# Input norm and HGRN value projection of a hybrid encoder trunk: one hand-written order, first channel halves of all token tiles ahead of the second

## The chip, the cores and the metric

The kernel runs on 1 core of one Trainium2 chip. The metric is device time in microseconds (us) of one execution; a comparison uses the median of several runs of each kernel. TensorE (PE, with its weight loads as PEld) does the matmuls and transposes, VectorE (DVE) and ScalarE (ACT) the elementwise work, GpSimd (POOL) some small operations, SyncE (SP) issues most DMAs.

## The reference, cut to what matters

One layer of an encoder: x (512 tokens x 1024 channels, float32) goes through a token mixer (HGRN2 heads and mLSTM heads), cross-attention over 256 memory tokens and a squared-ReLU MLP. The change touches only its beginning, the norm of the input and one block of columns of the input projection:

```python
def rmsnorm(x, g):
    y = x32 * lax.rsqrt(jnp.mean(x32 * x32, axis=-1, keepdims=True) + NORM_EPS)
    return (y * g.astype(jnp.float32)).astype(x.dtype)

# token_mixer(rmsnorm(x, norm_mix), ...)
proj = xn @ w_in + b_in            # w_in: 1024 x 4624
(h_q, h_f_fwd, h_f_bwd, h_i, h_g, m_q, m_k, m_v, m_o, ...) = split_cols(proj, IN_SPLITS)
v_h = to_heads(h_i, HGRN_HEADS)    # h_i: columns 1536 to 2047, the HGRN values
```

## The kernel before, in words

Every float32 matrix product is done as three matmuls on a high and a low part (L236, L237, L238): high by high, high by low, low by high. So each operand is first split: ACT copies it rounded (the high part), DVE subtracts that from the original (the low part). This is `split_out` (L232 on ACT, L233 on DVE).

Weights stream from one packed array in 512 KB slices. `load(i)` issues slice i on SP's queue into one of 3 buffers `st`; `split(i)` makes its pair `wh`, `wl`, of which there are also 3. The value projection uses slices 0 to 3: slice q holds the 256 input channels 2q and 2q+1 (in units of 128) for all 512 output columns. Slice 4 is that of the gates, slices 5 and on are those of the next projections.

The input norm works by token tiles t = 0 to 3 (128 tokens each) and channel halves g = 0, 1 (512 channels each). For a tile: ACT squares and sums it (L301), DVE (L172) and POOL (L174) make 1/rms; for each half, DVE scales it by 1/rms and by the gain (L306, the scale), PE turns it with four 128x128 transposes against the identity, which lies in the constants `cs` (L309, the turn), ACT and DVE split the result into `xT[g]` (L232, L233). The gain row is spread over the partitions by two small matmuls (L144) into `gmix`, two of the four PSUM banks of the pool `mm`. The value projection (`proj_t`, called behind the norm) takes four more banks of that pool, one for each token tile. Each (tile, slice) piece is six 128x512 matmuls: two channel blocks by three products. Slices 0 and 1 need `xT[0]` of that tile, slices 2 and 3 need `xT[1]`.

What sets the order: the program text is only a wish. A scheduler in the tile framework orders each engine's instructions by priority and by its own idea of when inputs are ready; the scale, the turn and the split are written under high priority. It is decided when the program is built. On the chip each engine then runs its own list strictly in that order, and waits on semaphores for the others. `small_setup` (masks, small constants, `selr` at L162 and L163) is also placed by that scheduler.

Of the kernel before, what the change touches and what calls it, by code (L numbers as in the profile page):

```python
# [13 lines left out]
AF = mybir.ActivationFunctionType  # L14
ALU = mybir.AluOpType
# [3 lines left out]
P = 128  # L19
S = 512  # L20
D = 1024
# [58 lines left out]
def trunk(ctx: ExitStack, tc: tile.TileContext, x, mem, wpk, vec, cst, lmask, rmask, rows, out):  # L80
# [5 lines left out]
    v, sc, gp, pe = nc.vector, nc.scalar, nc.gpsimd, nc.tensor  # L86
    cnt = [0]

    def nm(s):
        cnt[0] += 1  # L90
        return f"{s}_{cnt[0]}"

    def T(tag, w, bufs, dt=F32):
        return (sb if w == 516 else big).tile([P, w], dt, tag=tag, name=nm(tag), bufs=bufs)

    def mmb():
        return psm.tile([P, 512], F32, tag="mm", name=nm("mm"))

    def smb():
        return pss.tile([P, 512], F32, tag="sm", name=nm("sm"))  # L100

    def tiny(w):
        return sb.tile([P, w], F32, tag=f"tiny{w}", name=nm("tiny"), bufs=2 if w == 8 else 6)

    def ap(t, off, *dims):
        a = t[:, :]
        return bass.AP(a.tensor, a.offset + off, [list(a.ap[0])] + [list(d) for d in dims])
# [16 lines left out]
    ident = cs[:, C_ID:C_ID + P]  # L124
    grow1 = RG()
    xin = [A16(), A16()]
    xtile = [xin[t // 2][:, (t % 2) * 1024:(t % 2) * 1024 + 1024] for t in range(4)]
# [6 lines left out]
    def load_x(t):  # L134
        nc.sync.dma_start(out=xtile[t], in_=x[t * P:t * P + P, :])
# [3 lines left out]
    nc.scalar.dma_start(out=cs, in_=cst[:, 0:NC1])  # L139
    one1 = misc[0:1, 63:64]  # L140
    gp.memset(one1, 1.0)
    gmix = [mmb(), mmb()]
    for g in range(2):
        pe.matmul(gmix[g], lhsT=one1.to_broadcast([1, P]), rhs=grow1[0:1, g * 512:g * 512 + 512], start=True, stop=True)  # L144

    def small_setup():
        lmf = A4()
        nc.sync.dma_start(out=vc, in_=vec)
        nc.sync.dma_start(out=lmf[:, 0:len(LEVELS) * P], in_=lmask)
        for j in range(2):  # L150
            a = lmf[64 * j:64 * j + 64, 64 * j:NLV * P]
            v.tensor_copy(lm[64 * j:64 * j + 64, :].rearrange("p (l t) -> p l t", t=64),
                          bass.AP(a.tensor, a.offset, [list(a.ap[0]), [P, NLV], [1, 64]]))
        le, lr = tiny(8), tiny(8)
        lg = vc[:, V_LB:V_LB + 8]
        v.tensor_tensor(out=le, in0=lg, in1=lg, op=ALU.subtract)
        sc.activation(le, le, AF.Exp)
        v.reciprocal(lr, le)
        v.tensor_tensor(out=le, in0=le, in1=lr, op=ALU.mult)
        v.tensor_tensor(out=lb[:, 0:8], in0=le, in1=le, op=ALU.subtract)  # L160
        v.tensor_scalar(out=lb[:, 8:16], in0=lb[:, 0:8], scalar1=-1.0, scalar2=1.0, op0=ALU.mult, op1=ALU.add)
        v.tensor_copy(selr[0:64, :], cs[0:64, C_SEL:C_SEL + 8])  # L162
        v.tensor_copy(selr[64:128, :], cs[0:64, C_SEL:C_SEL + 8])  # L163
        v.tensor_scalar(out=negb, in0=vc[:, V_FF:V_FF + 8], scalar1=-1.0, scalar2=None, op0=ALU.mult)
# [5 lines left out]
    def rstd_of(ss, w, n):  # L170
        ms = tiny(w)
        v.tensor_scalar(out=ms, in0=ss, scalar1=1.0 / n, scalar2=EPS, op0=ALU.mult, op1=ALU.add)  # L172
        r = tiny(w)
        gp.tensor_tensor(out=r, in0=ms, in1=nh.to_broadcast([P, w]), op=ALU.pow)  # L174
        return r, ms
# [7 lines left out]
    def tick():  # L183
        for _ in range(rate[0]):
            tick1()
# [19 lines left out]
    st_tiles, hl_tiles = {}, {}  # L205

    def load(i):
        if i >= NSTREAM or i in st_tiles:
            return
        t = T("st", 1024, 3)  # L210
        nc.sync.dma_start(out=t, in_=wpk[i])
        st_tiles[i] = t

    def split(i):
        if i >= NSTREAM or i in hl_tiles:
            return
        load(i)
        s = st_tiles[i]
        hi, lo = T("wh", 1024, 3, F32R), T("wl", 1024, 3, F32R)
        split_out(hi, lo, s)  # L220
        hl_tiles[i] = (hi, lo)

    def weights(key):
        i = SIDX[key]
        with (tc.high_priority() if i > 2 else ExitStack()):
            for n in range(i, i + 3):
                split(n)
            load(i + 3)
        return hl_tiles[i]

    def split_out(dst_hi, dst_lo, src):
        sc.activation(dst_hi, src, AF.Copy)  # L232
        v.tensor_tensor(out=dst_lo, in0=src, in1=dst_hi.bitcast(F32), op=ALU.subtract)  # L233

    def mm3(ps, ah, al, bh, bl, first, last):
        pe.matmul(ps, lhsT=ah, rhs=bh, start=first, stop=False)  # L236
        pe.matmul(ps, lhsT=ah, rhs=bl, start=False, stop=False)  # L237
        pe.matmul(ps, lhsT=al, rhs=bh, start=False, stop=last)  # L238


    def xk(tiles, n=512):
        o = []
        for k in range(8):
            t = tiles[k // 4]
            b = (k % 4) * 2 * n
            o.append((t[:, b:b + n], t[:, b + n:b + 2 * n]))
        return o

    def proj_d(mat, c0, xs, n=512, count=2):

        for j in range(count):
            wh, wl = weights(("d", mat, 0, c0 + P * j))
            ps = mmb()
            for k in range(8):
                z = slice(k * P, k * P + P)
                mm3(ps[:, :n], wh[:, z], wl[:, z], xs[k][0], xs[k][1], k == 0, k == 7)
                if k == 3:
                    tick()
            yield ps
            tick()  # L260

    def proj_t(mat, k0, c0, xs, ntile=4, pre=None, late=False):

        acc = [mmb() for _ in range(ntile)]

        def part(t, q, w):
            for k in range(2):
                kk = 2 * q + k
                xh, xl = xs[kk][0][:, t * P:t * P + P], xs[kk][1][:, t * P:t * P + P]
                z = slice(k * 512, k * 512 + 512)  # L270
                mm3(acc[t], xh, xl, w[0][:, z], w[1][:, z], kk == 0, kk == 7)

        for q in range(2 if late else 3):
            w = weights(("t", mat, k0 + 2 * q, c0))
            for t in range(ntile):
                part(t, q, w)
                if t % 2 == 1:
                    tick()
        if pre is not None:
            pre()  # L280
        tail = [(q, weights(("t", mat, k0 + 2 * q, c0))) for q in range(2 if late else 3, 4)]
        for t in range(ntile):
            for q, w in tail:
                part(t, q, w)
            yield t, acc[t]
            if t % 2 == 1:
                tick()


    xT = XT()  # L290
    load(0)
    load_x(1)
    load_x(2)
    load(1)
    load_x(3)

    junk = G4()
    for t in range(4):
        xt = xtile[t]
        ss = tiny(1)  # L300
        sc.activation(junk, xt, AF.Square, accum_out=ss)  # L301
        r, _ = rstd_of(ss, 1, D)
        with tc.high_priority():
            for g in range(2):
                xg = xt[:, g * 512:g * 512 + 512]
                v.scalar_tensor_tensor(out=xg, in0=xg, scalar=r, in1=gmix[g], op0=ALU.mult, op1=ALU.mult)  # L306
                ps = smb()
                for k in range(4):
                    pe.transpose(ps[:, k * P:k * P + P], xg[:, k * P:k * P + P], ident)  # L309
                p3 = ps[:, :].rearrange("p (k t) -> p k t", t=P)  # L310
                split_out(ap(xT[g], t * P, [1024, 4], [1, P]), ap(xT[g], 512 + t * P, [1024, 4], [1, P]), p3)
        if t < 2:
            split(t)
    small_setup()
    xs = xk(xT)


    vh = []
# [1 line left out]
    def bias_row(i):  # L320
        b = T2()
        nc.sync.dma_start(out=b[:, 0:512], in_=rows[1 + i // 2:2 + i // 2, (i % 2) * 512:(i % 2) * 512 + 512].to_broadcast([P, 512]))
        return b

    bvh = bias_row(0)
    for t, ps in proj_t("in", 0, 1536, xs):
        d = VV()
        v.tensor_tensor(out=d[:, 0:512], in0=ps, in1=bvh[:, 0:512], op=ALU.add)
        vh.append(d)
# [431 lines left out]
    for t in range(2):  # L761
# [6 lines left out]
        ss = tiny(1)  # L768
        v.tensor_tensor(out=ss, in0=s2_[:, 0:1], in1=s2_[:, 1:2], op=ALU.add)
        r, _ = rstd_of(ss, 1, D)  # L770
# [6 lines left out]
    for k in range(8):  # L777
        ps = smb()
        for t in range(2):
            pe.transpose(ps[:, t * P:t * P + P], mt[t][:, k * P:k * P + P], ident)  # L780
        g = vc[:, V_MEM + k:V_MEM + k + 1]
# [224 lines left out]
    for f in range(4):  # L1006
# [3 lines left out]
        for p in range(4):  # L1010
            a = []
            for j in range(2):
                ps, = proj_d("up", 1024 * f + P * (p + 4 * j), x3, count=1)
# [49 lines left out]
        def ahead(n):  # L1063
            with tc.high_priority():
                for m in range(n, n + 3):
                    job(f, m)
                i = max(hl_tiles)
                for m in range(i + 1, i + 4):
                    load(m)
            if n == 8 and f < 3:  # L1070
                sum_loads(f + 1, ("U", "T3"))
            return job(f, n)
# [6 lines left out]
        while n < len(JOBS):  # L1079
            p, g = JOBS[n]  # L1080
# [8 lines left out]
            w = ahead(n)  # L1089
# [95 lines left out]
```

## Time and profile before

| | |
|---|---|
| median of 3 runs (lowest to highest) | 861.75 us (860.46 to 863.5) |
| the profiled execution: its own time | 861.91 us |
| its span, first to last instruction | 860.1 us |
| PE busy in the span | 840.4 us (98%) |
| DVE, ACT, POOL busy | 566.6, 423.7, 67.4 us |
| mean granted TensorE clock | 0.995 of full |
| first matmul of the value projection | 11.32 us after the span's start |

The kernel is bound by PE nearly everywhere. A row of the timeline gives start, duration, engine, line, operation, output and input, count, and in brackets how long the engine was idle just before and what ended that. PE's rows overlap, since matmuls are pipelined: what counts there is the distance from one start to the next, not the duration of one row.

### The profile page before, as it was taken

The page shows a single profiled execution, that of the slowest core. Times are in us where ns is not written, and L with a number is a line of the kernel's source. Part 1 is how long each engine was busy: PE and PEld are TensorE (multiplying, and loading weights), DVE is VectorE, ACT ScalarE, POOL GpSimd, SP SyncE. Part 2 cuts the span into 40 slices and gives each one's busy share as a digit, 9 for nine tenths or more (in the row PEclk, how much of TensorE's full clock was granted, in tenths as well). Part 3 has the DMA queues.
Part 4 walks back from the last instruction along what each step waited for, and adds up shares of the span by engine and source line. Part 5 has one row for each costly group of instructions (what it writes and reads, how often), then busy time and mean ns, then how long its engine had stood idle before and what let it go on. Part 6 is the DMA issues. An engine that isn't in the chain of part 4 may idle for free.

```text
span 860.1 us, 11677 instructions
## 1 busy us (share of the span) xinstructions
PE 840.4 (98%) x4438; PEld 693.8 (81%) x4438; DVE 566.6 (66%) x996; ACT 423.7 (49%) x773; POOL 67.4 (8%) x114
## 2 busy tenths in 40 slices
PE   7999999998999999999999999999999999999995
PEld 5888788887987987888888887888888888888884
DVE  5558874599347987654545446676667656856675
ACT  5336454445558576454443346553454344434544
POOL 1000000100010000100001200003101210220001
PEclk9999999999999999999999999999999999999998
DMA  7332223122152232452213852348935993698322
GB/s 265 123 119 75 73 80 136 46 94 76 50 147 74 99 123 99 158 135 98 74 50 110 206 149 76 97 130 229 282 118 127 275 259 99 173 284 203 123 50 98
DMA packets 32682, 113.62 MB, mean 132 GB/s; under 512 B 3761, under 2 KB 3889, under 8 KB 32626
## 3 DMA queue, kind: packets, MB, share of 16 engines
q1 hardware_dynamic: 23120, 78.84, 26.9%
q0 software_dynamic: 9216, 33.56, 17.7%
q8 instruction: 35, 0.57, 0.3%
q10 hardware_dynamic: 290, 0.47, 0.2%
q14 instruction: 21, 0.17, 0.1%
HBM read 110.76 MB, written 2.10 MB: 131 GB/s over the span
## 4 chain that ended last, share of the span: by engine, by line
PE 85%; issue 6%; DVE 5%; DMA 1%; ACT 1%; POOL 1%; POOLq 0%; ACTq 0%; DVEq 0%
PE mm L236 19%; PE mm L237 19%; PE mm L238 18%; PE sm L1059 5%; PE sm L1060 5%; PE sm L1061 5%; PE sm L688 2%; PE sm L673 2%; PE sm L454 2%; DVE wl L233 1%; PE sm L384 1%; PE mm L1060 1%; PE mm L1061 1%; PE mm L1059 1%; DVE a L479 1%
## 5 line engine op out<-in xcount | busy, mean ns | idle before, releaser
L232 ACT ACTIVATE wh<-st 128x1024 fp32r<-128x1024 f32 x133 | 141.1, 1061 | 223.2 <-PE mm L237 118.8
L233 DVE TENSOR_TENSOR wl<-st,wh 128x1024 fp32r<-128x1024 f32 x133 | 162.7, 1223 | 106.8 <-ACT wh L232 101.7
L236 PE MATMUL mm<-xT,wh 128*128 128x512 f32 x544 | 216.0, 398 | 0.0
L237 PE MATMUL mm<-xT,wh 128*128 128x512 f32 x544 | 213.2, 392 | 0.4 <-DVE xT L836 0.4
L238 PE MATMUL mm<-xT,wl 128*128 128x512 f32 x544 | 212.3, 390 | 0.0
L237 PEld LDWEIGHTS mm<-xT,wh 128*128 128x128 f32 x544 | 102.2, 188 | 22.9 <-DVE xT L836 2.0
L236 PEld LDWEIGHTS mm<-xT,wh 128*128 128x128 f32 x544 | 102.2, 188 | 22.2 <-issue 0.7
L238 PEld LDWEIGHTS mm<-xT,wl 128*128 128x128 f32 x544 | 102.1, 188 | 21.3 <-issue 0.2
L951 POOL DMA_DIRECT2D as<-in_wpk x48 | 36.5, 770 | 312.0 <-DVE wl L233 187.2
L1017 DVE SCALAR_TENSOR_TENSOR t<-mm,rg 128x512 f32<-128x512 f32 x32 | 22.1, 691 | 55.1 <-PE mm L238 55.0
L236 PE MATMUL mm<-wh,yT 128*128 128x512 f32 x128 | 50.6, 395 | 0.0
L238 PE MATMUL mm<-wh,yT 128*128 128x512 f32 x128 | 50.4, 394 | 0.0
L237 PE MATMUL mm<-wl,yT 128*128 128x512 f32 x128 | 50.4, 393 | 0.0
L1059 PE MATMUL sm<-wh,yT 128*128 128x512 f32 x128 | 49.8, 389 | 0.0
L1060 PE MATMUL sm<-wl,yT 128*128 128x512 f32 x128 | 49.8, 389 | 0.0
L1061 PE MATMUL sm<-wh,yT 128*128 128x512 f32 x128 | 49.8, 389 | 0.0
L232 ACT ACTIVATE wh<-as 128x1024 fp32r<-128x1024 f32 x24 | 25.5, 1062 | 33.3 <-PE sm L1061 23.7
L233 DVE TENSOR_TENSOR wl<-as,wh 128x1024 fp32r<-128x1024 f32 x24 | 29.4, 1226 | 13.7 <-ACT wh L232 13.7
L174 POOL TENSOR_TENSOR tiny<-tiny,misc 128x4 f32<-128x4 f32 (+1 forms) x14 | 11.9, 850 | 282.5 <-DVE tiny L172 282.5
L990 DVE TENSOR_TENSOR vv<-vv,sm 128x512 f32<-128x512 f32 x48 | 31.0, 680 | 1.2 <-PE sm L1061 1.2
L236 PEld LDWEIGHTS mm<-wh,yT 128*128 128x128 f32 x128 | 24.1, 188 | 5.3 <-DVE a L233 0.5
L232 ACT ACTIVATE yT<-t 128x512 fp32r<-128x512 f32 x32 | 19.8, 630 | 17.0 <-DVE t L1034 16.5
(275 smaller groups left out, 1510.5 us busy)
## 6 DMA issues: line engine op xcount, KB each, us to landing
st<-in_wpk SPq DMA_DIRECT2D x133, 512.0 KB, 3.3
as<-in_wpk POOLq DMA_DIRECT2D x48, 512.0 KB, 7.2
gate<-in_wpk POOLq DMA_DIRECT2D x16, 512.0 KB, 7.1
as<-in_x SPq DMA_DIRECT2D x4, 512.0 KB, 6.3
vv<-in_x SPq DMA_DIRECT2D x8, 256.0 KB, 4.2
out<-vv SPq DMA_DIRECT2D x7, 256.0 KB, 2.3
a<-in_mem SPq DMA_DIRECT2D x2, 512.0 KB, 5.1
t<-in_rows SPq DMA_DIRECT2D x2, 256.0 KB, 6.1
```

Source lines behind the costliest of these rows:

```text
L232: sc.activation(dst_hi, src, AF.Copy)
L233: v.tensor_tensor(out=dst_lo, in0=src, in1=dst_hi.bitcast(F32), op=ALU.subtract)
L236: pe.matmul(ps, lhsT=ah, rhs=bh, start=first, stop=False)
L237: pe.matmul(ps, lhsT=ah, rhs=bl, start=False, stop=False)
L238: pe.matmul(ps, lhsT=al, rhs=bh, start=False, stop=last)
L454: pe.matmul(ps[:, t * P:t * P + P], lhsT=A[j][:, s * 512 + t * P:s * 512 + t * P + P], rhs=vh[s][:, h * P:h * P + P], start=(s == 0), stop ...
L951: gp.dma_start(out=dst, in_=wpk[idx], **kw)
L990: v.tensor_tensor(out=z, in0=z, in1=ps, op=ALU.add if sign > 0 else ALU.subtract)
L1017: v.scalar_tensor_tensor(out=y, in0=ps, scalar=0.0, in1=rrow[:, 0:512], op0=ALU.max, op1=ALU.mult)
L1059: pe.matmul(ps, lhsT=ah, rhs=bh, start=new, stop=False, **fl)
L1060: pe.matmul(ps, lhsT=ah, rhs=bl, start=False, stop=False, **fl)
L1061: pe.matmul(ps, lhsT=al, rhs=bh, start=False, stop=end and k == 1, **fl)
```

## The change

Four things are changed, all in the first tens of microseconds.

1. The norm and three quarters of the value projection are written out as one list of steps, under high priority and with the scheduler switched off for PE, DVE and ACT: these three run the steps in the order of the text. The steps are `x_stat` (square, sum, 1/rms), `x_scale`, `x_turn`, `x_split` (each by tile and half), `part_v(t, q)` (the six matmuls of tile t with slice q) and `split(i)`. First the first halves of tiles 0 to 3 go through, with slices 0 and 1 between them, then the second halves, with slice 2. The last slice follows behind, scheduled as before.
2. The two gain rows `gmix` lie in the pool `sm` in place of `mm`, and the four banks of the projection are taken at once.
3. On SP's queue the second weight slice goes ahead of the third tile of x, and the third slice right behind the fourth tile; the vector of constants and the masks, and the bias row, change places with the weights.
4. `small_setup` stands at the end of the list; with it DVE's two copies into `selr` leave the start.

```diff
-    gmix = [mmb(), mmb()]
+    gmix = [smb(), smb()]
...
     load(0)
     load_x(1)
+    load(1)
     load_x(2)
-    load(1)
     load_x(3)
+    load(2)
 
     junk = G4()
-    for t in range(4):
-        xt = xtile[t]
+    rx, tp = {}, {}
+
+    def x_stat(t):
         ss = tiny(1)
-        sc.activation(junk, xt, AF.Square, accum_out=ss)
-        r, _ = rstd_of(ss, 1, D)
-        with tc.high_priority():
-            for g in range(2):
...
-        if t < 2:
-            split(t)
-    small_setup()
-    xs = xk(xT)
+        sc.activation(junk, xtile[t], AF.Square, accum_out=ss)
+        rx[t], _ = rstd_of(ss, 1, D)
...
+    acc_v = [mmb() for _ in range(4)]
+
+    def part_v(t, q):
+        w = hl_tiles[q]
+        for k in range(2):
+            kk = 2 * q + k
+            z = slice(k * 512, k * 512 + 512)
+            mm3(acc_v[t], xs[kk][0][:, t * P:t * P + P], xs[kk][1][:, t * P:t * P + P], w[0][:, z], w[1][:, z], kk == 0, kk == 7)
+
+    ET = mybir.EngineType
+    with tc.high_priority(), tc.manual_schedule(engines={ET.PE, ET.DVE, ET.Activation}):
+        x_stat(0)
+        x_scale(0, 0)
+        x_turn(0, 0)
+        split(0)
+        x_stat(1)
+        x_split(0, 0)
+        part_v(0, 0)
+        x_scale(1, 0)
+        x_turn(1, 0)
+        split(1)
+        x_stat(2)
+        part_v(0, 1)
+        x_split(1, 0)
+        x_scale(2, 0)
+        part_v(1, 0)
+        x_turn(2, 0)
+        x_stat(3)
+        part_v(1, 1)
+        x_split(2, 0)
+        x_scale(3, 0)
+        x_turn(3, 0)
+        part_v(2, 0)
+        x_scale(0, 1)
+        x_split(3, 0)
+        x_turn(0, 1)
+        part_v(2, 1)
+        split(2)
+        x_split(0, 1)
+        x_scale(1, 1)
+        part_v(3, 0)
+        x_turn(1, 1)
+        load(3)
+        x_split(1, 1)
+        x_scale(2, 1)
+        part_v(3, 1)
+        x_turn(2, 1)
+        part_v(0, 2)
+        x_split(2, 1)
+        x_scale(3, 1)
+        x_turn(3, 1)
+        part_v(1, 2)
+        x_split(3, 1)
+        part_v(2, 2)
+        split(3)
+        part_v(3, 2)
+        small_setup()
...
     bvh = bias_row(0)
-    for t, ps in proj_t("in", 0, 1536, xs):
+    load(4)
+    load(5)
+    for t, ps in enumerate(acc_v):
+        part_v(t, 3)
```

From the middle of the small chain of the gates (L545) on, the lists of all five engines are the same as before, instruction for instruction; up to there PE has the same matmuls and transposes in another order.

**DVE at the start.** The list of the kernel before; `as` is a tile of x, `tiny` its 1/rms, `wl` the low part of a weight slice, `xT` the low part of a turned half, the x128 shapes are per partition:

```order
L172 TENSOR_SCALAR tiny_97<-tiny_95 128x1
L162 CAST selr<-cs 64x8
L163 CAST selr<-cs 64x8
L233 TENSOR_TENSOR wl_118<-st_87,wh_117 128x1024
L306 SCALAR_TENSOR_TENSOR as_71<-as_71,tiny_99,mm_80 128x512
L306 SCALAR_TENSOR_TENSOR as_71<-as_71,tiny_99,mm_81 128x512
L172 TENSOR_SCALAR tiny_123<-tiny_121 128x1
L306 SCALAR_TENSOR_TENSOR as_71<-as_71,tiny_125,mm_80 128x512
```

The same place in the changed kernel, where L309 is the scale:

```order
L172 TENSOR_SCALAR tiny_105<-tiny_103 128x1
L309 SCALAR_TENSOR_TENSOR as_71<-as_71,tiny_107,sm_80 128x512
L233 TENSOR_TENSOR wl_116<-st_87,wh_115 128x1024
L172 TENSOR_SCALAR tiny_121<-tiny_119 128x1
L233 TENSOR_TENSOR xT_85<-sm_110,xT_85 128x4x128
L309 SCALAR_TENSOR_TENSOR as_71<-as_71,tiny_123,sm_80 128x512
```

The first scale moved ahead of the copies into `selr` and of the first weight split, and the scale of the second half left this place.

**PE at the third and fourth tile.** Before: L309 is a turn (four transposes), `as_72` holds tiles 2 and 3, `mm_209` to `mm_211` are the banks of token tiles 0 to 2, `wh_117` slice 0, `wh_143` slice 1, `wh_215` slice 2:

```order
L309 MATMUL sm_154<-cs,as_72 128x128 x4
L237 MATMUL mm_210<-wl_144,xT_85 128x512
L309 MATMUL sm_162<-cs,as_72 128x128 x4
L238 MATMUL mm_210<-wh_143,xT_85 128x512
L236 MATMUL mm_209<-wh_215,xT_86 128x512
L236 MATMUL mm_210<-wh_215,xT_86 128x512
L309 MATMUL sm_176<-cs,as_72 128x128 x4
L236 MATMUL mm_211<-wh_117,xT_85 128x512
L309 MATMUL sm_184<-cs,as_72 128x128 x4
L237 MATMUL mm_211<-wl_118,xT_85 128x512
```

Changed: L314 is a turn, `mm_98` and `mm_99` are the banks of token tiles 1 and 2, `wh_115` is slice 0 and `wh_139` slice 1:

```order
L314 MATMUL sm_164<-cs,as_72 128x128 x4
L236 MATMUL mm_98<-wh_139,xT_85 128x512
L237 MATMUL mm_98<-wl_140,xT_85 128x512
L238 MATMUL mm_98<-wh_139,xT_85 128x512
L236 MATMUL mm_98<-wh_139,xT_85 128x512
L237 MATMUL mm_98<-wl_140,xT_85 128x512
L238 MATMUL mm_98<-wh_139,xT_85 128x512
L314 MATMUL sm_184<-cs,as_72 128x128 x4
L236 MATMUL mm_99<-wh_115,xT_85 128x512
```

Four turns with single matmuls between them became one turn, six matmuls of one piece, the next turn.

**DVE at the same place.** Before, with the 1/rms and the scales of tiles 2 and 3:

```order
L306 SCALAR_TENSOR_TENSOR as_72<-as_72,tiny_151,mm_80 128x512
L306 SCALAR_TENSOR_TENSOR as_72<-as_72,tiny_151,mm_81 128x512
L172 TENSOR_SCALAR tiny_171<-tiny_169 128x1
L152 CAST lm<-a_35_191 64x384
L306 SCALAR_TENSOR_TENSOR as_72<-as_72,tiny_173,mm_80 128x512
```

Changed:

```order
L309 SCALAR_TENSOR_TENSOR as_72<-as_72,tiny_147,sm_80 128x512
L172 TENSOR_SCALAR tiny_171<-tiny_169 128x1
L233 TENSOR_TENSOR xT_85<-sm_164,xT_85 128x4x128
L309 SCALAR_TENSOR_TENSOR as_72<-as_72,tiny_173,sm_80 128x512
L309 SCALAR_TENSOR_TENSOR as_71<-as_71,tiny_107,sm_81 128x512
```

The scale of tile 3 now stands behind the low part of the turned tile 2 (`xT_85<-sm_164`), on the same engine.

## Rows read from the trace of the kernel before

**Rows 1.** Waits of PE over the whole span: total us, times, longest.

```profile
PE sm L309 <- DVE as L306: 2.5, 1, 2.5
PE sm L430 <- DVE a L479: 1.5, 1, 1.5
```

**Rows 2.** Busy us by engine in a stretch; then granted clock, DMA share, GB/s.

```profile
9.50:41.50 32.00, 31.98 (x145) 26.45 (x146) 21.37 (x37) 13.09 (x19) 3.28 (x10) 1.00 0.46 155
```

**Rows 3.** Timeline of PE, start to steady state: start us, duration us, instruction.

```profile
3.31 3.75 PE L144 MATMUL mm<-rg,misc 1*128 1x512 f32 x4 [3.31 <-DMA rg<-in_rows]
9.52 1.97 PE L309 MATMUL sm<-cs,as 128*128 128x128 f32 x8 [2.46 <-DVE as L306]
11.32 0.79 PE L236 MATMUL mm<-wh,xT 128*128 128x512 f32 x1
...
14.47 0.61 PE L238 MATMUL mm<-wh,xT 128*128 128x512 f32 x1
14.90 0.62 PE L309 MATMUL sm<-cs,as 128*128 128x128 f32 x4
...
16.29 0.39 PE L236 MATMUL mm<-wh,xT 128*128 128x512 f32 x1
16.52 0.39 PE L237 MATMUL mm<-wl,xT 128*128 128x512 f32 x1
```

**Rows 4.** Timeline of DVE, 7 to 15 us.

```profile
7.21 0.16 DVE L162 CAST selr<-cs 64x8 fp32r<-64x8 f32 x1 [1.38 <-DMA cs<-in_cst]
...
7.58 1.23 DVE L233 TENSOR_TENSOR wl<-st,wh 128x1024 fp32r<-128x1024 f32 x1
8.72 1.40 DVE L306 SCALAR_TENSOR_TENSOR as<-as,tiny,mm 128x512 f32<-128x512 f32 x2
...
10.85 0.75 DVE L306 SCALAR_TENSOR_TENSOR as<-as,tiny,mm 128x512 f32<-128x512 f32 x1 [0.67 <-POOL tiny L174]
11.52 0.68 DVE L233 TENSOR_TENSOR xT<-sm,xT 128x512 fp32r<-128x512 f32 x1
12.12 0.74 DVE L306 SCALAR_TENSOR_TENSOR as<-as,tiny,mm 128x512 f32<-128x512 f32 x1
...
14.06 0.69 DVE L233 TENSOR_TENSOR xT<-sm,xT 128x512 fp32r<-128x512 f32 x1 [0.55 <-ACT xT L232]
```

**Rows 5.** Timeline of POOL: 1/rms of the first tile.

```profile
5.91 0.56 POOL L174 TENSOR_TENSOR tiny<-tiny,misc 128x1 f32<-128x1 f32 x1 [4.94 <-DVE tiny L172]
```

**Rows 6.** Timeline of ACT, 4 to 20 us.

```profile
4.49 1.06 ACT L301 ACTIVATE gate<-as 128x1024 f32<-128x1024 f32 x1 [1.68 <-DMA as<-in_x]
...
7.64 1.06 ACT L301 ACTIVATE gate<-as 128x1024 f32<-128x1024 f32 x1 [0.65 <-DMA as<-in_x]
8.60 0.19 ACT L301 ACTIVATION_READ_ACCUMULATOR gate<-as 128x1 f32 x1
10.67 0.60 ACT L232 ACTIVATE xT<-sm 128x512 fp32r<-128x512 f32 x1 [1.88 <-PE sm L309]
...
13.43 0.60 ACT L232 ACTIVATE xT<-sm 128x512 fp32r<-128x512 f32 x1 [0.64 <-PE sm L309]
13.92 1.05 ACT L232 ACTIVATE wh<-st 128x1024 fp32r<-128x1024 f32 x1
...
19.65 1.27 ACT L232 ACTIVATE xT<-sm 128x512 fp32r<-128x512 f32 x2 [1.51 <-PE sm L309]
```

**Rows 7.** Timeline of PE at the third tile: turns between single matmuls.

```profile
19.02 0.60 PE L309 MATMUL sm<-cs,as 128*128 128x128 f32 x4
19.37 0.48 PE L237 MATMUL mm<-wl,xT 128*128 128x512 f32 x1
19.69 0.60 PE L309 MATMUL sm<-cs,as 128*128 128x128 f32 x4
```

**Rows 8.** The loads of x: issue of the fourth tile; landing times of all four.

```profile
3.35 0.48 SPq L135 DMA_DIRECT2D as<-in_x  x1
...
DMA to landing us min/median/max: 3.7/6.3/8.1
```

More of the change, by code (lines that the diff above doesn't have):

```diff
@@ L290, in trunk @@
     xT = XT()
+    xs = xk(xT)
     load(0)
     load_x(1)
+    load(1)
     load_x(2)
-    load(1)
     load_x(3)
+    load(2)
     junk = G4()
-    for t in range(4):
-        xt = xtile[t]
+    rx, tp = {}, {}
+    def x_stat(t):
         ss = tiny(1)
-        sc.activation(junk, xt, AF.Square, accum_out=ss)
-        r, _ = rstd_of(ss, 1, D)
-        with tc.high_priority():
-            for g in range(2):
[L305 to L311, printed above, removed]
-        if t < 2:
-            split(t)
@@ L314, in trunk, with x_scale, x_turn @@
-    small_setup()
-    xs = xk(xT)
+        sc.activation(junk, xtile[t], AF.Square, accum_out=ss)
+        rx[t], _ = rstd_of(ss, 1, D)
+    def x_scale(t, g):
+        xg = xtile[t][:, g * 512:g * 512 + 512]
+        v.scalar_tensor_tensor(out=xg, in0=xg, scalar=rx[t], in1=gmix[g], op0=ALU.mult, op1=ALU.mult)
+    def x_turn(t, g):
+        tp[t, g] = smb()
+        for k in range(4):
+            pe.transpose(tp[t, g][:, k * P:k * P + P], xtile[t][:, g * 512 + k * P:g * 512 + k * P + P], ident)
@@ new lines, in x_split @@
+    def x_split(t, g):
+        p3 = tp[t, g][:, :].rearrange("p (k t) -> p k t", t=P)
+        split_out(ap(xT[g], t * P, [1024, 4], [1, P]), ap(xT[g], 512 + t * P, [1024, 4], [1, P]), p3)
+    acc_v = [mmb() for _ in range(4)]
[5 more added lines that the diff above has]
+            mm3(acc_v[t], xs[kk][0][:, t * P:t * P + P], xs[kk][1][:, t * P:t * P + P], w[0][:, z], w[1][:, z], kk == 0, kk == 7)
```

## The prediction

> **What bounds the kernel now.** I read the waits of PE first. Over the whole span its longest wait behind a step that it depends on is one of 2.5 us for the first scaled tile, and the next one, far later, is 1.5 us and is a DVE chain, not a transfer [rows 1]. So PE is the bound, and time that PE loses at the start is not given back later by a transfer that lands early: it goes through to the end one for one. The windows say the same of the stretch that the change rewrites: from 9.5 to 41.5 us PE is busy 31.98 of 32.00 us [rows 2]. There is no gap in it to close. What the stretch can still give is an earlier first step, and time at the higher of TensorE's two clock levels.
>
> On both, PE's timeline is to be read by distances from start to start [rows 3]. The gain matmuls run from 3.31 us, the first turn starts at 9.52, the first matmul of the projection at 11.32. From 14.47 to 14.90 us, and ahead of it, a 512-column matmul takes 0.43 us, which is 1.2 GHz; from 16.29 to 16.52 it takes 0.23, which is 2.4 GHz. The granted clock reads 1.00 in that whole stretch [rows 2], so the level is read here from the distances. I put the rise at 15.0 us: 3.68 us after the first matmul of the projection, 5.48 after the first turn.
>
> **Part 1: the start.** The first turn waited for DVE, which waited at 7.21 us for the constants, made the two copies into `selr`, split the first weight slice (7.58) and scaled two halves from 8.72 on [rows 4]. Now the scale stands first. It needs 1/rms, which POOL ends at 5.91 + 0.56 = 6.47 [rows 5], and the first gain row. PE's four gain rows end at 3.31 + 3.75 = 7.06 [rows 3]; the first of the two matmuls is the first half of them, so I take 6.50, with 7.10 as the other end. A scale takes 0.74 (0.75 at 10.85) [rows 4], so it ends at 7.24, and the constants are there at 7.21 [rows 4]. The turn starts at 7.29, that is **2.23 us earlier**.
>
> But the next step of PE needs the high part of that half. ACT took it at 10.67, 1.15 after the turn began [rows 6]; now that would be 8.44, but ACT's list has the square of the second tile ahead of it, from 7.64 until 8.60 + 0.19 = 8.79 [rows 6]. So the high part runs from 8.81 to 9.41, and the first projection matmul starts at 9.46. The turn at four times some 0.21 (eight take 1.97) [rows 3] kept PE until 8.14, so PE idles **1.32 us**. Net, the start gives 2.23 - 1.32 = 0.91. If the scale starts at 7.10, the high part comes at 9.05 and 0.24 of that is lost.
>
> **Part 2: the clock.** Cold time costs half of itself. Before: 15.0 - 9.52 = 5.48 us of PE work at the lower level, 2.74 lost. If the rise again comes 3.68 us behind the first projection matmul, it comes at 13.14; PE works cold for 0.85 + 3.68 = 4.53, 2.27 lost. **Gain 0.47.** The ends: a rise at once at 9.46 (the gain matmuls and the first turn now follow each other closely) loses only 0.43, a gain of 2.3; a rise at 15.0 as before loses (0.85 + 5.54) / 2 = 3.2, a loss of 0.46.
>
> What the rows show is one execution, in which the projection matmuls from 11.32 to 14.90 us were cold. The Trainium skill, in "TensorE: Matmul & The Clock Gate", Part 1, says that the number of cold matmuls differs from run to run of one kernel, and advises not to fit a model to one count. By that the 0.47 would be left out and the sum below would come to 1.84; no run here shows the number vary.
>
> **Part 3: waits that the fixed order puts into PE's list.** This is the main term. In the new list PE has one turn, then one piece of six matmuls, then the next turn, and on DVE the scale for that next turn stands behind the low part of the previous one (the second and third places shown with the change). So from turn to turn runs a chain over three engines. Each link from start to start:
> - turn to high part 0.63 (19.02 [rows 7] to 19.65 [rows 6]);
> - high part to low part 0.63 (13.43 [rows 6] to 14.06 [rows 4]);
> - low part to scale 0.60 (11.52 to 12.12 [rows 4]);
> - scale 0.74 and 0.06 to PE (12.12 [rows 4]; 8.72 + 0.74 against 9.52 [rows 3, 4]).
>
> Together 2.66. PE's work in that time at the higher level: a turn and one matmul take 0.67 (19.02 to 19.69 [rows 7]), five more matmuls 5 x 0.227, together 1.81. PE waits 0.85. This holds for the turns of tile 3 in the first half and of tiles 2 and 3 in the second: the text has one piece between turn and turn there. At the turn of tile 2, first half, two pieces lie between, and part of them is cold, where six matmuls take 6 x 0.43 = 2.6. The turn of tile 0, second half, has its scale ready. That of tile 1, second half, is barely covered: with the third slice's split in its chain (7.58 to 8.72 on DVE [rows 4]) it comes 0.63 + 0.57 + 1.10 + 1.14 + 0.60 + 0.80 = 4.84 after the turn of tile 3, against two turns and three pieces on PE, 4.99. So **three waits, 2.55 us**. Before, two scales were made in a row and four turns stood among single matmuls, so PE always had something ready.
>
> **Part 4: the rest.** The last slice is split behind the low part of the last turn: from that turn 0.63 + 0.57 to the start of its high part, 1.05 + 0.05, and 1.23 for its low part (high part 13.92 [rows 6], low part 7.58 [rows 4]), 3.53 in all. PE has a turn and thirteen matmuls for it, 0.45 + 2.95 = 3.40. A wait of **0.2**; between 0 and 0.5, since scheduled work follows there. The second slice ahead of the third tile costs nothing: the loads of x landed 3.7 to 8.1 us after their issue, the last issued at 3.35 [rows 8], so all x is in by 11.45. The square of the third tile then starts no later than 11.5, its 1/rms is ready some 2 us later, and the scale of that tile waits until about 14.4 for the low part of the second one. If that cover goes, each microsecond beyond it costs one. The masks and constants, which now go behind the weights on SP's queue, are read only behind the norm. The gain rows take two banks of the turns' pool; two turns at a time are left, and PE never has more than two open. The projection gets its four banks at once; before, tiles 2 and 3 waited for the gain rows to end, but PE had no gap there [rows 2], so nothing is gained.
>
> **The sum.** -0.91 - 0.47 + 2.55 + 0.2 = +1.37 us. The profiled execution took 861.91, so 863.3; it lies 0.16 above the median of the runs shown, which I leave aside. With a rise between 11.2 us (1.4 gained) and 15.0, and the bounds of the small waits, the forecast's own range is 862.3 to 864.5.
>
> **The rivals.**
>
> *The clock rises early* (chance 0.16). PE works almost without a gap from 3.31 us now, where it idled 2.46 us ahead of the first turn [rows 3]. The gain is 2.3 in place of 0.47; but then the first pieces run ahead of their inputs: the first low part ends 0.27 too late, the low part of the second slice about as much. -0.91 - 2.3 + 0.5 + 2.55 + 0.2 = 0.0: 862.0. Against it: the same gain matmuls, which took 3.75 us, brought no rise before.
>
> *The clock rises late: slower* (0.16). The gap at 8.14 and the thinner matmuls around the turns hold the lower level longer. A rise at 17 us means (0.85 + 7.54) / 2 = 4.2 lost, 1.46 more than before: -0.91 + 1.46 + 2.55 + 0.2 = +3.3: 865.2. It decides from a rise at 15.6 us on: there the sum passes 2.6. For it: before, the rise came 5.48 us after the first turn, with PE never idle. Against it: projection matmuls now start 1.86 us earlier and stand closer together.
>
> *The waits are covered: faster* (0.13). If the chain from turn to turn is shorter than 1.81, or the steps overlap more than the list suggests, Part 3 falls away: -0.91 - 0.47 + 0.2 = -1.2: 860.7, and with an early rise, -2.5: 859.4. Against it: every link of the chain is a row, and PE takes nothing out of order. That the change does not do what it says I leave out, since the lists show it done.
>
> **How the numbers follow.** The forecast has 0.53; 0.02 is left for what I have not seen. About 0.3% (2.6 us) is what a measurement here can tell from no change. Slower by more than that: the late rise and the forecast's upper edge, 0.17. Faster by more: only waits covered and an early rise together, 0.05. Within: 0.78. The range that leaves out 2 in 10 takes in the early rise and most of the late one and of the covered waits: 860.7 to 865.3.
>
> **What would show it.** In the changed profile: the first turn near 7.3 us and the first projection matmul near 9.5, released by ACT; the distance of matmuls falling from 0.43 to 0.23 near 13; three idle times of PE of 0.85 ahead of turns (L314), released by the scale on DVE (L309), at about 18, 26 and 28 us; the first matmul of the gates some 1.4 us later in PE's work than before; the rest shifted by the same amount. I am wrong if these waits are missing or well under half a microsecond, if the clock rises beyond 15.6 or below 11 us, or if a wait for x appears on ACT ahead of 12 us that delays a turn.

## The result

The changed kernel takes 864.43 us (median of 22 runs, 862.33 to 865.65) against 862.08 (22 runs beside them, 860.01 to 863.54). The ratio is 1.0026, with a 95% interval from 1.0018 to 1.0035: 2.2 us slower, at most 3.0. The 2.2 lie inside what I had called "no change" (2.6 us), the end of the interval does not, and the sign is certain. The profiled execution took 864.32 us, with a span of 862.6.

The profile after, in the same views as [rows 1 to 3]. First the waits of PE over the whole span (total us, times, longest):

```profile
PE sm L314 <- DVE as L309: 1.8, 3, 0.8
PE sm L496 <- DVE a L545: 1.5, 1, 1.5
PE sm L450 <- ACT t L459: 1.1, 1, 1.1
PE mm L236 <- ACT xT L232: 1.0, 1, 1.0
PE sm L314 <- issue: 0.7, 1, 0.7
```

The 2.5 us ahead of the first turn [rows 1] are gone. In their place stand 1.0 for the high part (ACT L232) and four smaller waits of turns (L314): three for a scale on DVE (0.25 of it at the first turn), one marked "issue". The 1.5 and 1.1 us further down the span were there before.

The windows of the stretch of [rows 2] (busy us of PE, PEld, DVE, ACT, POOL; then granted clock, DMA share, GB/s) say how much of it is now idle:

```profile
9.50:41.50 32.00, 29.74 (x133) 23.28 (x133) 19.02 (x35) 11.90 (x18) 2.88 (x10) 1.00 0.40 147
```

PE had been busy for 31.98 of these 32.00 us; it now is for 29.74. PE's timeline shows where (start us, duration us, instruction, idle time ahead of it and what ended it):

```profile
7.34 1.11 PE L314 MATMUL sm<-cs,as 128*128 128x128 f32 x4 [0.25 <-DVE as L309]
9.48 0.79 PE L236 MATMUL mm<-wh,xT 128*128 128x512 f32 x1 [1.02 <-ACT xT L232]
...
13.48 0.63 PE L237 MATMUL mm<-wl,xT 128*128 128x512 f32 x1
13.91 0.46 PE L238 MATMUL mm<-wh,xT 128*128 128x512 f32 x1
14.21 0.40 PE L236 MATMUL mm<-wh,xT 128*128 128x512 f32 x1
14.44 0.40 PE L237 MATMUL mm<-wl,xT 128*128 128x512 f32 x1
...
17.89 0.40 PE L238 MATMUL mm<-wh,xT 128*128 128x512 f32 x1
19.02 0.63 PE L314 MATMUL sm<-cs,as 128*128 128x128 f32 x4 [0.73 <-issue]
...
25.66 0.40 PE L238 MATMUL mm<-wh,xT 128*128 128x512 f32 x1
26.83 0.63 PE L314 MATMUL sm<-cs,as 128*128 128x128 f32 x4 [0.77 <-DVE as L309]
...
28.45 0.40 PE L238 MATMUL mm<-wh,xT 128*128 128x512 f32 x1
29.61 0.63 PE L314 MATMUL sm<-cs,as 128*128 128x128 f32 x4 [0.77 <-DVE as L309]
```

The first turn starts 2.18 us earlier than in [rows 3], the first matmul of the projection 1.84 earlier. The distance of matmuls falls from 0.43 (13.48 to 13.91) to 0.23 (14.21 to 14.44); the one between, 0.30, is partly at each level, which puts the rise at 14.06. Read in the same way, the kernel before rose at 14.94 (both to some 0.02 us): from its turn at 14.90 [rows 3] to the next matmul is 0.38, where it is 0.35 at the higher level [rows 7] and 0.71 at the lower (here from 12.20 to 12.91). That matmul's row before:

```profile
15.28 0.48 PE L236 MATMUL mm<-wh,xT 128*128 128x512 f32 x1
```

At 19.02, 26.83 and 29.61 a turn starts 1.13, 1.17 and 1.16 us after the matmul ahead of it. Without a wait it is 0.23, so 0.90, 0.93 and 0.93 are lost (to 0.01). The idle times in brackets are shorter than that, since a matmul's end is modelled later than its successor could start; the distances are what counts. The turn at 19.02 is marked "issue", but the scale it reads is the first of the two in the row from 18.17 below, which at 0.74 us a scale ended at about 18.9, just ahead of it.

DVE shows why they came late, here for the first and the last of the three:

```profile
17.57 0.69 DVE L233 TENSOR_TENSOR xT<-sm,xT 128x512 fp32r<-128x512 f32 x1 [2.23 <-ACT xT L232]
18.17 1.40 DVE L309 SCALAR_TENSOR_TENSOR as<-as,tiny,sm 128x512 f32<-128x512 f32 x2
...
28.12 0.69 DVE L233 TENSOR_TENSOR xT<-sm,xT 128x512 fp32r<-128x512 f32 x1 [1.44 <-ACT xT L232]
28.73 0.74 DVE L309 SCALAR_TENSOR_TENSOR as<-as,tiny,sm 128x512 f32<-128x512 f32 x1
```

At 28.12 DVE had been idle for 1.44 us, waiting for ACT's high part, while the scale for the next turn stood behind it in DVE's order.

How much of this reaches the end? The same matmul later on, the first of four with 64x64 tiles, is a mark that both kernels share. Its row before, and then after:

```profile
68.29 0.46 PE L610 MATMUL sm<-cs,a 64*128 64x64 f32 x4
```

```profile
70.95 0.46 PE L676 MATMUL sm<-cs,a 64*128 64x64 f32 x4
```

It comes 2.66 us later, and the span is 2.5 us longer: nearly all that is lost by 71 us stays lost.

### The profile page after: what moved, and what is told of

Its sections match the earlier page's. It is cut to its first block, busy times and chain, and to the rows that moved or that the text cites. A ratio compares the mean times of both kernels' runs of the same rounds, so it can differ in the third digit from the quotient of the medians.

```text
span 862.6 us, 11675 instructions
## 1 busy us (share of the span) xinstructions
PE 841.8 (98%) x4438; PEld 693.2 (80%) x4438; DVE 566.8 (66%) x996; ACT 423.4 (49%) x773; POOL 67.5 (8%) x114
## 4 chain that ended last, share of the span: by engine, by line
PE 50%; DVE 1%; issue 0%; ACT 0%; POOL 0%; POOLq 0%
PE mm L237 10%; PE mm L238 10%; PE mm L236 10%; PE sm L1125 5%; PE sm L1127 5%; PE sm L1126 5%; PE mm L1125 1%; PE mm L1127 1%; PE mm L1126 1%; PE sm L238 1%; PE sm L237 1%; PE sm L236 1%; PE sm L896 0%; PE sm L953 0%; ACT t L882 0%
## 5 line engine op out<-in xcount | busy, mean ns | idle before, releaser
L232 ACT ACTIVATE wh<-st 128x1024 fp32r<-128x1024 f32 x133 | 140.8, 1060 | 214.1 <-PE mm L237 127.1
L232 ACT ACTIVATE wh<-as 128x1024 fp32r<-128x1024 f32 x24 | 25.5, 1061 | 33.3 <-PE sm L1127 23.7
L232 ACT ACTIVATE yT<-t 128x512 fp32r<-128x512 f32 x32 | 19.8, 629 | 17.0 <-DVE t L1100 16.5
```

## The experiments

All kernels are the changed one with the edit shown, set against the kernel before, run beside them. "Mark" is the start of the matmul just named, 70.95 in the changed kernel; "rise" is read from the distances as above, 14.06 there. What the lower level costs is taken as half of PE's time from the first projection matmul to the rise, since a matmul takes 0.43 at one level and 0.23 at the other; in the changed kernel that time is 9.48 to 14.06, 4.58 us.

**1. The scale of the next turn ahead of the low part.** Three steps move up in the list; nothing else changes.

```
         x_stat(3)
+        x_scale(3, 0)
         part_v(1, 1)
         x_split(2, 0)
-        x_scale(3, 0)
...
-        x_split(1, 1)
         x_scale(2, 1)
+        x_split(1, 1)
...
-        x_split(2, 1)
         x_scale(3, 1)
+        x_split(2, 1)
```

> Only the place of three scales on VectorE is changed: that of tile 3 in the first half, and of tiles 2 and 3 in the second, each stands one step earlier, ahead of the low part of the turn before it. PE's order is that of the changed kernel. If the three waits of PE (0.90, 0.93 and 0.93 us, 2.76 in all) come from the place of these scales, they go and the time falls by 2.8 us from that of the changed kernel, to 861.7, 0.4 us below the kernel before. If the waits come from the turn and the split themselves, or if PE loses the same time further on, the time stays within 0.5 us of 864.4.

Measured: 861.19 us (12 runs), ratio 0.9997 (0.9987 to 1.0007). The loss is gone. What is left of PE's waits for a scale, and the turn that had started at 28.45 + 1.16 in the changed kernel:

```profile
PE sm L314 <- DVE as L309: 0.3, 1, 0.3
```

```profile
26.97 0.40 PE L238 MATMUL mm<-wh,xT 128*128 128x512 f32 x1
27.21 0.60 PE L314 MATMUL sm<-cs,as 128*128 128x128 f32 x4
```

The turn follows at a distance of 0.24. The one wait of a turn that is left is that of the first. The mark comes at 68.54, 2.41 earlier. Three waits are 2.76; a turn behind a wait also takes 0.38 to its next matmul (26.83 to 27.21) in place of 0.35, 0.09 for three. The projection begins at 9.29, 0.19 earlier in this execution, but the clock rises at 15.14 only (distances of 0.43, 0.29 and 0.23 from 14.58 on): 5.85 us at the lower level, 1.27 more, which cost 0.64. Together -2.76 - 0.09 - 0.19 + 0.64 = -2.40. So the order of two steps on DVE, and not the channel-half order itself, is what made the change slower.

**2. A fourth wait of the same kind.**

```
-        x_scale(0, 1)
         x_split(3, 0)
+        x_scale(0, 1)
         x_turn(0, 1)
```

> One more scale is put behind the low part of the turn before it: that of tile 0, second half, where the changed kernel has it ready. If a chain from turn to turn costs PE 2.79 us against 1.85 us of its own work, a fourth wait of 0.9 us appears ahead of the turn of tile 0, second half, and the time rises by 0.9 us from 864.4 to 865.3. If waits at the start are given back by slack further on, the wait appears and the time does not rise.

Measured: 865.49 us (5 runs), ratio 1.0047 (1.0026 to 1.0067). The new wait is where it was put, with the size of the others (1.17 - 0.23 = 0.94):

```profile
20.26 0.40 PE L238 MATMUL mm<-wh,xT 128*128 128x512 f32 x1
21.43 0.63 PE L314 MATMUL sm<-cs,as 128*128 128x128 f32 x4 [0.77 <-DVE as L309]
```

The mark comes 0.61 later: 0.94 + 0.03 for the wait, less 0.07 for a projection that begins at 9.41, less half of the 0.63 by which the time at the lower level is shorter (the rise is at 13.36); that makes 0.59. The price of the mechanism holds when it is added as when it is taken away.

**3. The start undone: the weight split first again.**

```
         x_stat(0)
+        split(0)
         x_scale(0, 0)
         x_turn(0, 0)
-        split(0)
```

> The early start is undone alone: the first weight slice is split ahead of the first scale, as in the kernel before. The first turn then starts at about 9.1 us in place of 7.34, and the first projection matmul, behind turn and high part, at about 10.9 in place of 9.48. If the start is worth what PE's first projection matmul gains, the time rises by 1.4 us, to 865.8. If the rise of the clock does not move with it and stays at 14.0 us, the lower level costs 0.7 us less and the time rises by 0.7 only, to 865.1. If ScalarE's square of the second tile is what holds the first projection matmul, and not the scale, it stays at 9.5 and nothing changes.

Measured: 865.82 us (4 runs), ratio 1.0050 (1.0032 to 1.0067).

```profile
9.04 1.11 PE L314 MATMUL sm<-cs,as 128*128 128x128 f32 x4 [2.10 <-DVE tiny L172]
10.85 0.79 PE L236 MATMUL mm<-wh,xT 128*128 128x512 f32 x1 [0.69 <-ACT xT L232]
```

The first turn comes 1.70 later, but the projection only 1.37 later, since PE's gap behind the turn shrinks. The mark moves by 1.17, to 72.12: the clock rises at 15.13, after 4.28 us at the lower level in place of 4.58, which gives back 0.15 of the 1.37; 0.05 stays open. So the early scale did bring a gain, and it is the projection's first matmul that tells its size, not the turn.

**4. Work for PE that nothing reads.** Does the clock's rise depend on what PE does ahead of the projection? Seven 128x512 matmuls of zeros go into a spare bank, four ahead of the gain matmuls, three behind the first turn.

```
+    spin(4)
     one1 = misc[0:1, 63:64]
...
         x_turn(0, 0)
+        spin(3)
         split(0)
```

> Added are seven 128x512 matmuls of zeros into a bank that is not read: four from about 1.6 us on, ahead of the gain rows, and three in the 1.3 us between the first turn and the first projection matmul, so that PE works without a gap from 1.6 us on. They are over by 9.48 us and hold nothing up. If the rise of the clock depends on how long PE has been at work, it comes earlier than at 14.0 us: at 9.5 it gives back up to 2.3 us, less some 0.5 us for first pieces that then run ahead of their inputs, 862.6; at 11.7 it gives 1.1 us, 863.3. If it comes at the same 14 us whatever PE did ahead of 9.5, nothing changes: 864.4.

Measured: 862.31 us (10 runs), ratio 1.0014 (1.0002 to 1.0026).

```profile
12.12 0.63 PE L323 MATMUL sm<-cs,as 128*128 128x128 f32 x4
12.51 0.48 PE L245 MATMUL mm<-wh,xT 128*128 128x512 f32 x1
12.83 0.40 PE L246 MATMUL mm<-wl,xT 128*128 128x512 f32 x1
```

The projection starts at 9.46, as in the changed kernel, and the clock rises at 12.19, 1.87 earlier. The mark comes 0.92 earlier, half of that, with the waits of the turns still there. Each microsecond by which the rise comes earlier is worth half a one. That the zeros brought it forward takes more than this one execution; experiments 6 and 8 bear on it. By the ratios the run is 0.12% faster than the changed kernel, with intervals that overlap.

**5. The first high part ahead of the second square on ACT**, on top of experiment 1:

```
         split(0)
-        x_stat(1)
         x_split(0, 0)
+        x_stat(1)
```

> The three scales stand one step earlier as in the run with the scales ahead, and on ScalarE the high part of the first turned half stands ahead of the square of the second tile. If that square is what holds the first projection matmul, it starts at 8.45 + 0.6 + 0.05 = 9.1 us in place of 9.3 to 9.5, PE's gap behind the first turn shrinks from 1.3 to 0.9 us, and the time falls by 0.2 to 0.4 us below that run, to 860.9, 0.8 below the kernel before. If the square of the second tile, which now ends near 10.2, then holds the second turn (it needs its scale at 11.7), the gain is lost again there and the time stays at 861.2.

Measured: 861.44 us (11 runs), ratio 0.9999 (0.9989 to 1.0009). ACT's row shows that the order did what it should: the high part ran at 8.41, where it had run at 8.85 behind the square.

```profile
8.41 0.60 ACT L232 ACTIVATE xT<-sm 128x512 fp32r<-128x512 f32 x1 [1.40 <-PE sm L314]
8.91 1.05 ACT L304 ACTIVATE gate<-as 128x1024 f32<-128x1024 f32 x1
```

The projection starts at 9.06, and the mark comes at 67.94, 0.35 ahead of the kernel before and 0.60 ahead of experiment 1: 0.23 by the earlier start, 0.37 by a rise at 14.18 (5.12 us at the lower level in place of 5.85). Over the runs such a third of a microsecond is lost in the scatter; this one is no more than "same".

**6. Experiment 5 and zeros together** (four and two matmuls):

> The same as the run with the high part first, with six matmuls of zeros added ahead of the projection (four from 1.5 us on, two between the first turn and the first projection matmul). If PE kept at work lets the clock rise near 12 us, as in the run with the zeros alone, against 14 to 15 us without, it gives 0.9 to 1.5 us more: 859.7, 2.0 us below the kernel before. If the rise seen there was chance, it comes at 13.4 to 15.1 us as in the others, and the time is that of the run without zeros, 860.9.

Measured: 860.79 us (11 runs), ratio 0.9992 (0.9983 to 1.0001). The clock rises at 11.47 and the mark comes at 67.43, 0.86 ahead of the kernel before and 3.5 ahead of the changed one. It is less than expected, because PE now runs ahead of DVE. A matmul waits for the low part of the second weight slice, which DVE ends at 11.72 + 1.22 = 12.94 (PE's rows, then DVE's; the bracket names a small step that DVE ended next and that this matmul does not read):

```profile
12.27 0.47 PE L245 MATMUL mm<-wh,xT 128*128 128x512 f32 x1
12.99 0.50 PE L246 MATMUL mm<-wl,xT 128*128 128x512 f32 x1 [0.25 <-DVE tiny L181]
```

```profile
11.72 1.22 DVE L242 TENSOR_TENSOR wl<-st,wh 128x1024 fp32r<-128x1024 f32 x1
```

That distance is 0.72, where 0.31 stands after a turn when nothing is waited for: 0.4 given back. The order of experiment 5 has its part in it. There the square of the second tile comes later on ACT, so its scale and this low part come later on DVE, from 11.57 on in experiment 5 and from 11.72 here; in experiment 8, without that order, the low part starts at 10.62, and no matmul waits for it although the clock rises earlier still. The zeros with the order of experiment 1 alone were not run. This version has the lowest ratio of all, 0.34% below the changed kernel by the two ratios; against the kernel before its interval just touches 1, and it overlaps those of experiments 1 and 5.

**7. The second slice behind the third tile again.**

```
-    load(1)
     load_x(2)
+    load(1)
```

> The changed kernel with one part undone: the second weight slice is loaded behind the third tile of x again. If the order of the loads costs and gains nothing, as the prediction has it, the first projection matmul, the three waits and the first matmul behind the second slice stay where they are within 0.1 us, and the time is 864.4 within its spread of 862.3 to 865.7. If the second slice is late, ScalarE's split of it starts near 10.8 us in place of 9.3, and a wait of PE appears ahead of the second piece of tile 0, near 12.9 us, of up to 0.7 us.

Measured: one run, 865.41 us. The projection starts at 9.55, the waits of the turns stand as in the changed kernel, and the mark comes at 70.64, 0.31 earlier, which a rise at 13.36 explains (half of 0.77 us less at the lower level, against 0.07 for the later start). The slice did come later: ACT starts its split at 10.33 in place of 9.32, and DVE ends its low part at 12.65. But PE reads that at 13.47 only, so the order of the loads did nothing that can be seen in the time. With a rise as early as in experiment 8, where PE reads it at 12.36, it would cost some 0.3 (an estimate from the times of these two runs).

**8. Zeros in the gap alone.** Three matmuls behind the first turn, none ahead of the gains:

```
         x_turn(0, 0)
+        spin(3)
         split(0)
```

> The changed kernel with only three matmuls of zeros, in the 1.3 us between the first turn and the first projection matmul. If that gap is what holds the lower clock level, the rise comes near 12 us, as with all seven; if the work ahead of the gain rows matters, or the rise is chance, it comes at 13.4 to 15.1 us, as in the kernels without zeros.

Measured: one run, 863.47 us. The rise:

```profile
10.83 0.54 PE L245 MATMUL mm<-wh,xT 128*128 128x512 f32 x1
11.21 0.40 PE L246 MATMUL mm<-wl,xT 128*128 128x512 f32 x1
11.44 0.40 PE L247 MATMUL mm<-wh,xT 128*128 128x512 f32 x1
```

10.83 to 11.21 is 0.38, then 0.23: the clock rises at 11.16, 2.90 earlier than in the changed kernel and earlier than with seven matmuls. The mark comes at 69.56, 1.39 earlier, against 1.45 for half of 2.90. So work in the gap is enough; that the four ahead of the gains add anything isn't shown, since a single execution of each is too little for that (below). Over all profiles, the clock rose at 11.16, 11.47 and 12.19 in the three kernels with zeros and between 13.36 and 15.14 in the seven without. The two groups do not overlap, so keeping PE busy does bring the rise forward; by how much in a given execution, three profiles do not say.

## Why the prediction was right, and where not

The forecast was +1.37 us, the profiled executions differ by 2.41, the medians by 2.35; 864.43 lies at the upper edge of the forecast's own range, 862.3 to 864.5. The mechanism was right, and two terms of the sum were mis-sized, the clock and the rest, both in the same direction, so the sum did not come near by errors that cancel. Each term, predicted and measured:

| term | predicted | measured | from |
|---|---|---|---|
| first turn earlier | -2.23 | -2.18 | 9.52 to 7.34 |
| gap ahead of the projection | +1.32 | +1.29 | 8.19 (7.34 + 0.85) to 9.48 |
| clock | -0.47 | 0.0 | 5.42 us of PE work at 1.2 GHz before, 0.85 + 4.58 = 5.43 after |
| three waits of turns | +2.55 | +2.76 | 0.90 + 0.93 + 0.93 |
| last slice, and the rest | +0.2 | +0.8 | what is left of 2.66 at the mark |
| sum | +1.37 | +2.66 | 68.29 to 70.95 |

The 0.85 for a turn at the lower level holds: with one matmul behind it a turn takes 1.28 (12.20 to 13.48), less 0.43.

**The start** was right to 0.05 in each half. The scale started at 6.54, where I had taken 6.50 with 7.10 as the other end, and ACT's high part stood behind the square as said (DVE's row, then ACT's):

```profile
6.54 0.75 DVE L309 SCALAR_TENSOR_TENSOR as<-as,tiny,sm 128x512 f32<-128x512 f32 x1 [0.68 <-POOL tiny L174]
```

```profile
8.75 0.19 ACT L304 ACTIVATION_READ_ACCUMULATOR gate<-as 128x1 f32 x1
8.85 0.58 ACT L232 ACTIVATE xT<-sm 128x512 fp32r<-128x512 f32 x1
```

With the square out of the way (experiment 5) the high part comes 0.44 earlier, and the projection 0.23 to 0.42.

**The waits**, the main term, were right in number, place and cause, and 0.05 to 0.08 each too small: from the turn at 26.83 to that at 29.61 the chain takes 2.78, where the links of [rows 4, 6, 7] added up to 2.66. Experiments 1 and 2 take them away and add one, with the price read here. The rival in which the chain is covered is ruled out by both.

**The clock** is the first of the two that were mis-sized. I carried 3.68 us from the first projection matmul to the rise over from one execution; here it was 4.58, and the gain vanished. The runs show why it could not be carried over: the changed kernel and those of experiments 1, 2 and 7, whose PE runs the same instructions in the same order up to the rise, rose at 14.06, 15.14, 13.36 and 13.36 us. That is 1.8 us apart, 0.9 us of time, with the projection starting within 9.29 to 9.55 in all four. The rule that I weighed in Part 2 and did not follow, that of the Trainium skill's "TensorE: Matmul & The Clock Gate", Part 1, agrees with these traces; the sum without that term, 1.84, would have been nearer. The rival of an early rise had the right mechanism but needs work in the gap to come true (experiments 4 and 8). The rival of a late rise did not come in any of the profiles: none rose as late as 15.6.

**The rest** was too small by 0.6. PE's weight loads (PEld) have waits of their own, which the list of PE's waits leaves out. From 30 us to the mark the kernel before has one, marked "issue", which the changed one has too. The changed kernel has five more. The longest three:

```profile
33.14 0.19 PEld L237 LDWEIGHTS mm<-wl,xT 128*128 128x128 f32 x1 [0.28 <-DVE wl L233]
41.82 0.19 PEld L238 LDWEIGHTS mm<-xT,wl 128*128 128x128 f32 x1 [0.32 <-DVE wl L233]
48.23 0.19 PEld L236 LDWEIGHTS mm<-xT,wh 128*128 128x128 f32 x1 [0.26 <-ACT wh L232]
```

Each is released by the split of a weight slice. The matmul at 33.14 is followed after 0.34 in place of 0.23, which loses 0.11, and that at 48.24 likewise. At 41.25 three transposes and a matmul take 0.91 to the next one, some 0.35 more than without a wait (one transpose and a matmul take 0.34 from 44.23, each further transpose 0.11). A shorter wait at 31.88 costs 0.06. That makes 0.6. The first of the three is the wait for the last slice, which I had put at 0.2; the other two I had not. Experiment 1 has all three, 2.4 us earlier, which fits a mark that is still 0.25 behind that of the kernel before. No experiment takes them away, and why these splits come so late against PE's new order stays open.

The turns behind the three waits for a scale add 0.09, as said. And from 14 to 40 us the matmuls of the projection stand 0.230 us apart, on the mean of 57 distances, where it was 0.227 on 82 before; that makes 0.2 to 0.3. This goes with the breaks in the order: from 16 to 50 us the first nine distances behind a turn or a wait are 0.231 on the mean in either kernel (19 of them before, 69 after), the later ones 0.227 before (101) and 0.228 after (32). Why a matmul takes longer shortly behind a break, these runs don't show. Together these parts come to some 0.9, where the table has 0.8.

## What to carry over

In a list written by hand, look on each engine for a step that one engine waits for (the next turn's scale) standing behind a step that itself waits for a third (the low part, waiting for ACT's high part): the chain then goes around all engines once per turn, and PE idles for the difference between the chain and its own work. Add up the links from start to start and compare with PE's work between two turns; that was good to a tenth of a microsecond here. Look at the waits of the weight loads too: a slice that is split too late shows there and not among PE's own waits. A term for the clock's rise, on the other hand, is worth only a bound when it comes from one execution.

## What the hardware showed

In most executions the granted clock falls once more, in the middle of the kernel and whatever the version. In the windows from 212 to 224 us (columns as above; the clock is the third number from the end) the changed kernel, that of experiment 4 and that of experiment 7 read:

```profile
212.00:224.00 12.00, 9.42 (x76) 8.72 (x75) 8.86 (x19) 8.20 (x18) 0.00 (x0) 0.86 0.13 45
```

```profile
212.00:224.00 12.00, 9.65 (x78) 8.93 (x79) 7.84 (x17) 7.28 (x18) 0.00 (x0) 1.00 0.12 44
```

```profile
212.00:224.00 12.00, 9.43 (x60) 8.36 (x55) 8.55 (x18) 7.30 (x17) 0.00 (x0) 0.72 0.15 45
```

A mean of 0.86 over 12 us is 3.4 us at the lower level, 0.72 is 6.7, and in the second there is none. The kernel before reads 0.86 too. It begins at these two idle times of PE, shown from the changed kernel, or up to some 1.7 us behind them (in experiment 2 the pairs of matmuls behind them start 0.22 apart at first and 0.42 apart from 218.27 on). The other profiles have both idle times too:

```profile
213.59 0.69 PE L450 MATMUL sm<-a,t 128*64 128x64 f32 x16 [1.05 <-ACT t L459]
215.80 0.77 PE L496 MATMUL sm<-a,a 128*128 128x128 f32 x2 [1.53 <-DVE a L545]
216.36 0.63 PE L497 MATMUL sm<-a,a 128*128 128x128 f32 x2
216.79 0.63 PE L496 MATMUL sm<-a,a 128*128 128x128 f32 x2
```

The pairs of matmuls behind them start 0.43 apart here; in experiment 4, behind the same two idle times, they start 0.22 apart at once:

```profile
214.87 0.46 PE L506 MATMUL sm<-a,a 128*128 128x128 f32 x2 [1.51 <-DVE a L555]
215.17 0.39 PE L507 MATMUL sm<-a,a 128*128 128x128 f32 x2
215.39 0.39 PE L506 MATMUL sm<-a,a 128*128 128x128 f32 x2
```

Over the runs it sorts the times: the 22 runs of the changed kernel have a mean clock of 0.997 (862.3 to 862.8 us), 0.995 (864.0 to 865.0) or 0.992 (865.0 to 865.7), and those of the kernel before fall into groups of the same kind, 860.0 to 860.7 at 0.997 and 861.3 to 862.2 at 0.995 beside experiments 1 to 4. The profiles with 0.993 to 0.995 are those with 3.4 us at the lower level there, the one with 0.997 has none, the one with 0.992 has 6.7; so most of the scatter of either kernel goes with this one place, and two kernels are best compared within a group. What decides in which executions the clock falls there, these runs don't show.
